# Accumulator banks handed out in pairs, one maximum over two heads, values split by one instruction each: a hybrid encoder trunk on one NeuronCore

## The chip, the core and the metric

The kernel runs on 1 core of one Trainium2 chip. The metric is device time in microseconds of one execution; before the change it is 1155.11 us, the median of 3 runs (1154.3 to 1155.8). The engines are TensorE (PE: matmuls and transposes), VectorE (DVE), ScalarE (ACT), GpSimd (POOL) and SyncE (SP, which here only starts transfers).

## What is computed

A two-layer encoder over 512 positions of 1024 channels, all in float32:

```python
h = layer_norm(x, ln_in_g, ln_in_b)
for l in range(2):
    a_in, b_q, b_k, b_v, c_in, d_cq, d_ckv, d_kr = split(h @ w_in[l])
    o_a = silu(layer_norm(depthwise_conv31(a * sigmoid(gate))))
    o_b = attention(rope(rms(q)), rope(rms(k)), v)      # 4 heads of 64, 2 for k and v
    o_c = u * (sgu_w @ layer_norm(sv) + sgu_b)          # c_in through gelu
    o_d = attention(q_full, k_full, v_d)                # 4 heads, 64 + 32 wide, low rank
    h = layer_norm(ALPHA * h + concat(o_a, o_b, o_c, o_d) @ w_out[l])
    up = depthwise_conv3(h @ ffn_w_up[l])               # 2 x 2816 wide
    h = layer_norm(ALPHA * h + (silu(up[:, :2816]) * up[:, 2816:]) @ ffn_w_down[l])
```

An attention is `softmax(q k^T * scale) v` over all 512 positions.

## The kernel before, in words

Every float32 operand of a product is split into a high part (rounded to fp32r) and a low part, the difference. A product is then three matmuls, high x high, high x low and low x high (`mm3`, line 733). `split` (line 739) makes the parts: ACT copies the high part, DVE (POOL for some weights) subtracts for the low part. Weights come from memory in chunks (`load`, line 668) and are split the same way; their tiles are `raw`, `wh` and `wl`. The normalised stream lies in `hh` and `hl`.

Sums are built in PSUM. There are two kinds of tiles for it, four of each: `acc` (method `acc`, line 659) and `wk`, each 128 partitions x 512 float32.

- In the attention, `att_scores` (line 1178) takes two `acc` tiles, one for each of two heads, and fills them by 6 matmuls in one group. `att_probs` (line 1187) takes the negated maximum of each head's scores on DVE (`max`) and then the exponential with its sum on ACT (`prob`). This is done for 2 x 4 query tiles in the B heads and as often in the D heads, in each layer. Then `att_transpose` and `att_pv` multiply the probabilities with the values.
- The values `bv` and `dv` are read from a `wk` tile in `b_evac` (line 1009) and `d_up` (line 1118): ACT copies the high part of each head, DVE subtracts for the low part, in the order in which the two heads' halves of a PSUM result need them.
- The up-projection `ffn` (line 1340) goes over 22 pairs of 128 columns. For pair `i`, `col_mm` (line 847) puts 24 matmuls, in four groups of 6, into the first tile (the part that goes through silu) and 24 into the second (its factor). Even pairs from 2 on take `wk` tiles, odd ones `acc` tiles. The first two pairs (`split_pairs`) take `acc` tiles and are done in halves of 256 columns. `up_pair` (line 1321) reads each tile three times: ACT with bias and scale (tile `y`), then two DVE `scalar_tensor_tensor` of 511 columns for the neighbours of the convolution. What follows (silu, product, split) reads no PSUM.
- The output projection and the down-projection are `residual` (line 1274): in each half of the columns four `acc` tiles, one for each 128 positions. The first chunks of weights go to all four in turn; the last chunk (in the second half the last four or five) is done for one tile after the other, and DVE adds each finished tile to `h`.

The order of the work is made before anything is issued. Each call on an engine is recorded (`record`, line 378) with the instructions that it must follow; `access` (line 417) works that out from the parts of a tile that are read and written. `place` (line 490) then plays the engines forward with a cost for each instruction (`cost`, line 445), free slots of each kind of tile (`SLOTS`) and priorities: the place in the program plus a number from the table `TUNE`. `issue` writes the instructions out in that order, and there the tile framework adds the waits that each instruction has in the built program:

```python
pool, n = self.pools[a.kind]
a.real_tile = pool.tile(a.full, a.dt, tag=f"{a.kind}{a.slot}", name=a.name, bufs=1)
```

All instructions are issued from one line (610, after the change 619), so rows are told apart by their tiles.

Of the kernel before, what the change touches and what calls it, by code (L numbers as in the profile page):

```python
# [9 lines left out]
F32 = mybir.dt.float32  # L10
# [6 lines left out]
P = 128  # L17
# [31 lines left out]
for _k in KEYS:  # L49
# [7 lines left out]
SLOTS = {"u": 69, "raw": 3, "acc": 4, "wk": 4, "s": 48}  # L57
# [14 lines left out]
TUNE = {'window': 334,  # L72
         'slack': 0.0,
         'spare': 1,
         'ahead': {'A': 6,
                   'B': 10,
                   'D': 10,
                   'U': 21,
                   'V': 12,
                   'C': 44,  # L80
                   'O': 5,
                   'F': 2,
                   'W': 6,
                   'W1': 35,
                   'W0': 15,
                   'C0': 42,
                   'A1': 17,
                   'V0': 17,
                   'C1': 42,
                   'F1': 6,  # L90
                   'A0': 30,
                   'B1': 34,
                   'D0': 9,
                   'F0': 5,
                   'B0': 27,
                   'V1': 28,
                   'U1': 32,
                   'U0': 40,
                   'D1': 5},
         'lead': {'A': 32,  # L100
                  'B': 14,
                  'D': 45,
                  'U': 73,
                  'V': 8,
                  'C': 0,
                  'O': 5,
                  'F': 37,
                  'W': 8,
                  'D1': 5,
                  'A0': 11,  # L110
                  'U1': 69,
                  'C1': 11,
                  'O1': 0,
                  'D0': 22,
                  'B1': 15,
                  'F1': 16,
                  'O0': 2,
                  'U0': 84,
                  'V1': 15,
                  'V0': 15,  # L120
                  'C0': 13,
                  'B0': 3,
                  'F0': 45,
                  'A1': 30,
                  'W0': 14,
                  'W1': 6},
         'rank': {'.0': 23,
                  '.1': -404,
                  '.3': -339,
                  'a0': 33,  # L130
                  'a1': 72,
                  'a_norm0': -14,
                  'b0': -1,
                  'b0.0': -212,
                  'b0.1': 256,
                  'b0.2': 81,
                  'b0.3': -477,
                  'b1': -618,
                  'b1.2': -365,
                  'b1.3': 59,  # L140
                  'b_att0': 142,
                  'b_att0.00': -455,
                  'b_att0.01': 19,
                  'b_att0.0n': 962,
                  'b_att0.10': -33,
                  'b_att0.1n': 49,
                  'b_att1': 24,
                  'b_att1.00': -25,
                  'b_att1.01': -10,
                  'b_att1.1n': 8,  # L150
                  'b_heads0': -527,
                  'b_heads0.0': 159,
                  'b_heads0.1': -3,
                  'b_heads1': 182,
                  'b_heads1.0': -174,
                  'b_heads1.1': -110,
                  'b_heads1.2': -4,
                  'b_rope0': -265,
                  'b_rope1': 794,
                  'c0': 78,  # L160
                  'c0.0': -15,
                  'c0.1': 6,
                  'c0.3': -638,
                  'c1': -66,
                  'c1.0': -131,
                  'c1.1': -9,
                  'c1.3': 150,
                  'c_norm0': 237,
                  'c_norm1': -16,
                  'c_sgu0': -22,  # L170
                  'c_sgu1': -283,
                  'conv0': 854,
                  'conv0.1': -86,
                  'conv1.0': -162,
                  'd0.0': 372,
                  'd0.2': -163,
                  'd1': 7,
                  'd1.0': -183,
                  'd1.1': 270,
                  'd1.2': 216,  # L180
                  'd1.3': -49,
                  'd_att0': -2,
                  'd_att0.20': 11,
                  'd_att0.21': 95,
                  'd_att0.2n': 135,
                  'd_att0.30': -186,
                  'd_att0.31': 5,
                  'd_att0.3n': 4,
                  'd_att1': -419,
                  'd_att1.20': 302,  # L190
                  'd_att1.21': -1797,
                  'd_att1.30': -317,
                  'd_att1.31': -134,
                  'd_att1.3n': 49,
                  'd_lat0': -141,
                  'd_norm1': 19,
                  'd_up1': -91,
                  'down0': -2632,
                  'down0.0': 365,
                  'down0.1': 5,  # L200
                  'down0.2': -346,
                  'down0.3': 3,
                  'down1': 13,
                  'down1.0': -52,
                  'down1.1': 1,
                  'down1.2': -16,
                  'down1.3': -54,
                  'ffn0': 194,
                  'ffn1': -7,
                  'out0': 12,  # L210
                  'out0.0': -4,
                  'out0.2': 243,
                  'out0.3': 221,
                  'out1.1': -12,
                  'out1.2': 40,
                  'out1.3': 34,
                  'tables0': -660,
                  'tables1': 62}}
# [104 lines left out]
class Sched:  # L323
# [121 lines left out]
    def cost(eng, method, args, kw, outs, ins):  # L445
# [27 lines left out]
        if eng == "ACT":  # L473
            from_psum = any(psum(v) for v in ins)
            return ((50.0 if from_psum else 94.0) + n / 1.2 + 72.0 * ptrs + (115.0 if "accum_out" in kw else 0.0),
                    118.0 if from_psum else 95.0, False)
# [3 lines left out]
        return 150.0 + n * (1.66 if narrow and n == 512 else 2.1), 40.0, True  # L480
# [141 lines left out]
class Kern:  # L622
    def __init__(self, ctx, tc, x, wst, sguw, pp, rows, tabs, incol, out):
# [26 lines left out]
        self.loaded = {}  # L650
# [8 lines left out]
    def acc(self):  # L659
        return self.s.tile("acc", [P, 512], F32, "acc")  # L660
# [348 lines left out]
    def b_evac(self, l):  # L1009
# [4 lines left out]
        def evac(t, ps):  # L1014
# [5 lines left out]
            v = self.unit([P, 2, P], FR, nm="bv")  # L1020
            pv = ps[:, 384:512].rearrange("p (h c) -> p h c", c=64)
            for i in range(2):
                s.ACT.activation(v[:, i, 64 * i:64 * i + 64], pv[:, i, :], AF.Copy)
            s.ACT.activation(y, pq, AF.Copy)
            for i in range(2):
                s.DVE.tensor_sub(v[:, i, 64 - 64 * i:128 - 64 * i], pv[:, i, :], v[:, i, 64 * i:64 * i + 64].bitcast(F32))
            self.bv.append(v)
            self.by.append(y)
        return evac

    def b_rope(self):

        s = self.s
# [497 lines left out]
```

## Time and profile before

| what | value |
|---|---|
| runs | 1154.3, 1155.8, 1155.11 us |
| profiled execution, device time | 1155.01 us |
| its span in the profile | 1153.2 us |
| instructions in the span | 15412 |
| mean granted clock of PE | 0.998 |

The span runs from the first to the last instruction that the profiler saw; the device time has a little more around it. A busy share is the time in which an engine had an instruction under way. Matmuls are pipelined, so one matmul's duration is longer than the step from its start to the next one's start. PEclk is the clock granted to PE as a share of 2.4 GHz. "idle before, releaser" gives the idle time of an engine just before an instruction and what ended it.

### The profile page before, as it was taken

How to read it: one execution, taken by the hardware profiler on the slowest of the kernel's cores; microseconds unless marked ns; L12 is line 12 of the kernel's file. 1: busy time of each engine (PE TensorE's matmuls, PEld its weight loads, DVE VectorE, ACT ScalarE, POOL GpSimd, SP SyncE). 2: the span in 40 equal slices, each digit the busy share in tenths (PEclk: the TensorE clock that was granted, in tenths of full speed). 3: DMA queues.
4: the chain of work that ended last, by engine and by line, in shares of the span. 5: the costliest groups of instructions: out<-in, count | busy, mean ns of one | idle time of the engine just before them, and what ended most of it. 6: DMA issues, size and time to landing. Idle time of an engine off the chain costs nothing.

```text
span 1153.2 us, 15412 instructions
## 1 busy us (share of the span) xinstructions
PE 1131.9 (98%) x5802; PEld 959.7 (83%) x5802; DVE 771.0 (67%) x1307; ACT 558.2 (48%) x1203; POOL 169.4 (15%) x203
## 2 busy tenths in 40 slices
PE   6999999999999999999999999999999999999997
PEld 5888888988888888888889877889888888888886
DVE  7799996776666755245667999777776656551425
ACT  5759794254444543224254679733564444431221
POOL 5324324100000001000112734320000000000002
PEclk9999999999999999999999999999999999999999
DMA  6520022233233532135232002122353223231311
GB/s 228 165 74 20 19 92 74 74 97 104 92 92 109 167 106 79 55 110 166 95 124 68 7 20 58 53 92 73 128 164 111 92 92 110 74 110 42 105 56 73
DMA packets 32041, 105.71 MB, mean 92 GB/s; under 512 B 3680, under 2 KB 4064, under 8 KB 31968
## 3 DMA queue, kind: packets, MB, share of 16 engines
q1 hardware_dynamic: 31968, 104.74, 27.7%
q8 instruction: 45, 0.74, 0.3%
q14 instruction: 28, 0.23, 0.1%
HBM read 102.63 MB, written 2.10 MB: 91 GB/s over the span
## 4 chain that ended last, share of the span: by engine, by line
PE 90%; ACT 5%; DVE 2%; DMA 1%; issue 1%; POOL 0%; SPq 0%; DVEq 0%; ACTq 0%
PE acc L610 55%; PE wk L610 35%; ACT prob L610 2%; ACT pth L610 1%; ACT wh L610 1%; DVE ptl L610 1%; ACT c L610 1%; DVE aconv L610 0%; DMA raw<-in_wst_dram 0%; DMA h<-in_x_dram 0%; ACT do L610 0%; DVE max L610 0%; DVE bo L610 0%; ACT mixh L610 0%; ACT bo L610 0%
## 5 line engine op out<-in xcount | busy, mean ns | idle before, releaser
L610 DVE TENSOR_TENSOR wl<-raw,wh 128x512 fp32r<-128x512 f32 (+1 forms) x264 | 171.6, 688 | 85.6 <-ACT wh L610 60.6
L610 ACT ACTIVATE wh<-raw 128x512 fp32r<-128x512 f32 (+2 forms) x310 | 176.1, 615 | 67.8 <-DMA raw<-in_wst_dram 60.8
L610 PE MATMUL acc<-hh,wh 128*128 128x512 f32 (+1 forms) x544 | 191.8, 353 | 0.0
L610 PE MATMUL acc<-hh,wl 128*128 128x512 f32 (+1 forms) x544 | 191.2, 352 | 0.0
L610 PE MATMUL acc<-hl,wh 128*128 128x512 f32 (+1 forms) x544 | 191.2, 352 | 0.0
L610 PE MATMUL wk<-hh,wh 128*128 128x512 f32 x320 | 124.5, 389 | 0.0
L610 PE MATMUL wk<-hl,wh 128*128 128x512 f32 x320 | 124.5, 389 | 0.0
L610 PE MATMUL wk<-hh,wl 128*128 128x512 f32 x320 | 124.5, 389 | 0.0
L610 PEld LDWEIGHTS acc<-hh,wl 128*128 128x128 f32 x544 | 102.8, 189 | 13.8
L610 PEld LDWEIGHTS acc<-hl,wh 128*128 128x128 f32 x544 | 102.9, 189 | 13.6
L610 PEld LDWEIGHTS acc<-hh,wh 128*128 128x128 f32 x544 | 102.9, 189 | 13.6
L610 POOL TENSOR_TENSOR vr<-ve,mhalf 128x1 f32<-128x1 f32 (+2 forms) x26 | 25.4, 977 | 534.6 <-DVE ve L610 534.5
L610 DVE SCALAR_TENSOR_TENSOR y<-acc,pp,y 128x511 f32<-128x511 f32 x96 | 71.6, 749 | 37.2 <-ACT y L610 35.4
L610 DVE TENSOR_TENSOR hl<-raw,hh 128x512 fp32r<-128x512 f32 x56 | 37.7, 689 | 84.3 <-ACT hh L610 84.2
L610 ACT ACTIVATE hh<-raw 128x512 fp32r<-128x512 f32 x56 | 34.9, 630 | 111.5 <-PE acc L610 93.5
L610 DVE SCALAR_TENSOR_TENSOR aconv<-aglu,pp,aconv 128x501 f32<-128x501 f32 (+14 forms) x120 | 86.7, 758 | 0.6
L610 PE MATMUL acc<-hl,fh 128*128 128x512 f32 x224 | 85.8, 383 | 0.0
L610 PE MATMUL acc<-hh,fh 128*128 128x512 f32 x224 | 85.7, 383 | 0.0
L610 PE MATMUL acc<-hh,fl 128*128 128x512 f32 x224 | 85.7, 382 | 0.0
L610 DVE SCALAR_TENSOR_TENSOR y<-wk,pp,y 128x511 f32<-128x511 f32 x80 | 60.0, 750 | 33.7 <-ACT y L610 31.9
L610 PE MATMUL wk<-wh,hh 128*128 128x512 f32 (+1 forms) x192 | 73.7, 384 | 0.0
L610 POOL TENSOR_TENSOR wl<-raw,wh 128x512 fp32r<-128x512 f32 (+1 forms) x46 | 59.8, 1320 | 91.6 <-ACT wh L610 58.3
(201 smaller groups left out, 2290.5 us busy)
## 6 DMA issues: line engine op xcount, KB each, us to landing
raw<-in_wst_dram SPq DMA_DIRECT2D x172, 512.0 KB, 3.5
row<-in_rows_dram SPq DMA_DIRECT2D x16, 256.0 KB, 5.0
raw<-in_wst_dram SPq DMA_DIRECT2D x8, 352.0 KB, 3.0
out_dram<-h SPq DMA_DIRECT2D x8, 256.0 KB, 2.0
h<-in_x_dram SPq DMA_DIRECT2D x3, 512.0 KB, 5.2
raw<-in_wst_dram SPq DMA_DIRECT2D x2, 384.0 KB, 3.8
h<-in_x_dram SPq DMA_DIRECT2D x2, 256.0 KB, 3.1
raw<-in_wst_dram SPq DMA_DIRECT2D x2, 256.0 KB, 3.1
```

What stands on the lines that cost most here:

```text
L610: f(*[a.real() if isinstance(a, View) else a for a in args], **{k: v.real() if isinstance(v, View) else v for k, v in kw.items()})
```

## The change

1. `acc` hands out halves: every second call makes one tile of 128 x 1024 and returns its first half, the next call returns the second half. `SLOTS` goes from 4 to 2 of them.
2. `att_probs` takes one maximum over both halves (128 x 2 x 512 to 128 x 2); the exponentials stay one a head.
3. The four 64-column parts of a pair of heads lie side by side as high, low, low, high, so one ACT copy writes both high parts and one DVE subtraction both low parts (`bv`; for `dv` both pairs of heads at once).
4. `cost` counts less for the sum beside an exponential and other amounts for POOL; the table `TUNE` (a window, a slack, how early chunks are loaded and split, ranks of sections) is set anew.

```diff
-SLOTS = {"u": 69, "raw": 3, "acc": 4, "wk": 4, "s": 48}
+SLOTS = {"u": 69, "raw": 3, "acc": 2, "wk": 4, "s": 48}
...
-TUNE = {'window': 334,
-         'slack': 0.0,
+TUNE = {'window': 528,
+         'slack': 62.7,
...
-            return ((50.0 if from_psum else 94.0) + n / 1.2 + 72.0 * ptrs + (115.0 if "accum_out" in kw else 0.0),
+            return ((50.0 if from_psum else 94.0) + n / 1.2 + 72.0 * ptrs + ((30.0 if n == 512 else 115.0) if "accum_out" in kw else 0.0),
...
     def acc(self):
-        return self.s.tile("acc", [P, 512], F32, "acc")
+
+        if self.acc_next is None:
+            pair = self.s.tile("acc", [P, 1024], F32, "acc")
+            self.acc_next = pair[:, 512:1024]
+            return pair[:, 0:512]
+        half, self.acc_next = self.acc_next, None
+        return half
...
-            v = self.unit([P, 2, P], FR, nm="bv")
+            v = self.unit([P, 4, 64], FR, nm="bv")
             pv = ps[:, 384:512].rearrange("p (h c) -> p h c", c=64)
-            for i in range(2):
-                s.ACT.activation(v[:, i, 64 * i:64 * i + 64], pv[:, i, :], AF.Copy)
+            s.ACT.activation(v[:, 0:4:3, :], pv, AF.Copy)
             s.ACT.activation(y, pq, AF.Copy)
-            for i in range(2):
-                s.DVE.tensor_sub(v[:, i, 64 - 64 * i:128 - 64 * i], pv[:, i, :], v[:, i, 64 * i:64 * i + 64].bitcast(F32))
-            self.bv.append(v)
+            s.DVE.tensor_sub(v[:, 1:3, :], pv, v[:, 0:4:3, :].bitcast(F32))
+            self.bv.append([v[:, 2 * i:2 * i + 2, :].rearrange("p a c -> p (a c)") for i in range(2)])
...
-            v = self.unit([P, 2, 2, P], FR, nm="dv")
+            v = self.unit([P, 2, 4, 64], FR, nm="dv")
...
+            hi = v[:, :, 0:4:3, :]
+            s.ACT.activation(hi, pv, AF.Copy)
+            s.DVE.tensor_sub(v[:, :, 1:3, :], pv, hi.bitcast(F32))
...
         m, ps = self.small([P, 2], nm="max"), []
+        s.DVE.tensor_reduce(m, sc[0].t.rearrange("p (h n) -> p h n", h=2), AX.X, ALU.max, negate=True)
         for j in range(2):
-            s.DVE.tensor_reduce(m[:, j:j + 1], sc[j], AX.X, ALU.max, negate=True)
             p = self.unit([P, S], nm="prob")
```

In instructions of the built program: PE keeps its 5804 rows; DVE has 32 maxima instead of 64, and 16 subtractions for `bv` and `dv` instead of 32; ACT has 16 copies for them instead of 32. POOL and SP keep theirs.

**The order on PE in the up-projection.** Layer 0, pair 5, with the waits of the built program; the number behind a name tells one buffer from another. Before, the last two matmuls of the first tile (`acc_671`), the first group of 6 into the second tile (`acc_672`) and the beginning of its second group:

```order
L610 MATMUL acc_671_3189<-hl_88,wh_676_3059 128x512
L610 MATMUL acc_671_3189<-hh_87,wl_677_3063 128x512
L610 MATMUL acc_672_3233<-hh_87,wh_679_3091 128x512 [waits PE_49,Activation_49]
L610 MATMUL acc_672_3233<-hl_88,wh_679_3091 128x512
L610 MATMUL acc_672_3233<-hh_87,wl_680_3101 128x512 [waits DVE_49]
L610 MATMUL acc_672_3233<-hh_87,wh_679_3091 128x512
L610 MATMUL acc_672_3233<-hl_88,wh_679_3091 128x512
L610 MATMUL acc_672_3233<-hh_87,wl_680_3101 128x512
L610 MATMUL acc_672_3233<-hh_87,wh_679_3091 128x512
L610 MATMUL acc_672_3233<-hl_88,wh_679_3091 128x512
L610 MATMUL acc_672_3233<-hh_87,wl_680_3101 128x512
L610 MATMUL acc_672_3233<-hh_87,wh_679_3091 128x512
```

With the change, from the last matmul into the first half of `acc_644` on: the first group of 6 into its second half, and the beginning of the second group:

```order
L619 MATMUL acc_644_3150<-hh_87,wl_649_2936 128x512
L619 MATMUL acc_644_3150<-hh_87,wh_651_2969 128x512
L619 MATMUL acc_644_3150<-hl_88,wh_651_2969 128x512
L619 MATMUL acc_644_3150<-hh_87,wl_652_2979 128x512
L619 MATMUL acc_644_3150<-hh_87,wh_651_2969 128x512
L619 MATMUL acc_644_3150<-hl_88,wh_651_2969 128x512
L619 MATMUL acc_644_3150<-hh_87,wl_652_2979 128x512
L619 MATMUL acc_644_3150<-hh_87,wh_651_2969 128x512 [waits DVE_49]
L619 MATMUL acc_644_3150<-hl_88,wh_651_2969 128x512
L619 MATMUL acc_644_3150<-hh_87,wl_652_2979 128x512
L619 MATMUL acc_644_3150<-hh_87,wh_651_2969 128x512
L619 MATMUL acc_644_3150<-hl_88,wh_651_2969 128x512
```

Before, the second tile's waits stand at its first use of a weight's high and low part. Now the first matmul of the second group waits for DVE; the count that it waits for is that of the first `y_655` row below. The first matmul of the third group, six rows on, waits for DVE again, for the count of the second `y_655` row.

**The order on DVE at the same place.** The subtractions for weights (`wl`) and the convolution of the pair. Before:

```order
L610 TENSOR_TENSOR wl_709_3231<-raw_705_3198,wh_708_3227 128x512 [waits Activation_49]
L610 SCALAR_TENSOR_TENSOR y_683_3240<-acc_671_3189,pp_89,y_683_3240 128x511 [waits Activation_49]
L610 SCALAR_TENSOR_TENSOR y_683_3240<-acc_671_3189,pp_89,y_683_3240 128x511 [waits DVE_49]
L610 TENSOR_TENSOR wl_712_3269<-raw_710_3242,wh_711_3259 128x512 [waits DMAHW0_49,Activation_49]
L610 TENSOR_TENSOR wl_714_3271<-raw_710_3242,wh_713_3267 128x512 [waits Activation_49]
L610 SCALAR_TENSOR_TENSOR y_684_3280<-acc_672_3233,pp_89,y_684_3280 128x511 [waits Activation_49]
```

With the change:

```order
L619 TENSOR_TENSOR wl_696_3192<-raw_692_3159,wh_695_3188 128x512 [waits Activation_49]
L619 SCALAR_TENSOR_TENSOR y_655_3200<-acc_644_3150,pp_89,y_655_3200 128x511 [waits Activation_49]
L619 SCALAR_TENSOR_TENSOR y_655_3200<-acc_644_3150,pp_89,y_655_3200 128x511 [waits DVE_49,PE_49]
L619 TENSOR_TENSOR wl_699_3229<-raw_697_3202,wh_698_3219 128x512 [waits DMAHW2_49,Activation_49]
L619 TENSOR_TENSOR wl_701_3231<-raw_697_3202,wh_700_3227 128x512 [waits Activation_49]
L619 SCALAR_TENSOR_TENSOR y_656_3240<-acc_644_3150,pp_89,y_656_3240 128x511 [waits Activation_49]
```

The rows stand in the same order. The second `y_655` row waits for PE too, for the count of the last matmul of the second half's second group. ACT's `y_655`, which the first one waits for, waits for PE in both kernels: before for the last matmul of its tile, now for the last one of the second half's first group.

**The order on DVE in the attention.** Layer 0, the third and fourth query tile of a D pair. Before, two heads' maxima with other work between them:

```order
L610 TENSOR_REDUCE max_397_1797<-acc_395_1754 128x1 [waits PE_49]
L610 TENSOR_TENSOR ptl_383_1801<-wk_381_1773,pth_382_1787 128x512 [waits Activation_49]
L610 TENSOR_TENSOR ptl_386_1812<-wk_384_1780,pth_385_1799 128x512 [waits Activation_49]
L610 TENSOR_TENSOR dl_436_1821<-wk_434_1747,dh_435_1803 96x512 [waits Activation_49]
L610 TENSOR_REDUCE max_397_1797<-acc_396_1755 128x1
L610 TENSOR_TENSOR ptl_390_1839<-wk_388_1807,pth_389_1827 128x512 [waits Activation_49]
L610 TENSOR_REDUCE max_402_1850<-acc_400_1789 128x1
```

With the change:

```order
L619 TENSOR_REDUCE max_382_1769<-acc_381_1745 128x2 [waits PE_49]
L619 TENSOR_TENSOR ptl_369_1790<-wk_367_1762,pth_368_1776 128x512 [waits Activation_49]
L619 TENSOR_TENSOR ptl_372_1801<-wk_370_1771,pth_371_1783 128x512 [waits Activation_49]
L619 TENSOR_TENSOR ptl_376_1805<-wk_374_1778,pth_375_1792 128x512 [waits Activation_49]
L619 TENSOR_TENSOR ptl_379_1814<-wk_377_1785,pth_378_1803 128x512 [waits Activation_49]
L619 TENSOR_REDUCE max_386_1822<-acc_385_1794 128x2 [waits PE_49]
```

One row now gives both heads' maxima, and both heads' exponentials stand behind it.

## Rows read from the trace of the kernel before

**Rows 1.** The page's first part: busy time, share of the span, instructions, by engine.

```profile
PE 1131.9 (98%) x5802; PEld 959.7 (83%) x5802; DVE 771.0 (67%) x1307; ACT 558.2 (48%) x1203; POOL 169.4 (15%) x203
```

**Rows 2.** The chain of work that ended last, shares of the span by engine.

```profile
PE 90%; ACT 5%; DVE 2%; DMA 1%; issue 1%; POOL 0%; SPq 0%; DVEq 0%; ACTq 0%
```

**Rows 3.** Stretches: busy PE, PEld, DVE, ACT, POOL (instructions), PEclk, DMA share, GB/s.

```profile
10.00:20.00 10.00, 7.46 (x32) 5.46 (x32) 7.63 (x15) 4.57 (x9) 8.69 (x8) 0.88 0.77 286
20.00:30.00 10.00, 10.00 (x51) 8.26 (x51) 9.69 (x20) 8.23 (x36) 3.30 (x6) 0.95 0.28 112
129.00:168.00 39.00, 36.56 (x243) 31.54 (x242) 37.26 (x75) 38.43 (x92) 15.59 (x13) 1.00 0.25 82
241.00:448.00 207.00, 207.00 (x915) 171.39 (x914) 135.08 (x198) 96.84 (x159) 3.72 (x4) 1.00 0.34 110
666.00:730.00 64.00, 61.06 (x393) 50.62 (x392) 61.27 (x113) 57.40 (x129) 19.41 (x22) 1.00 0.19 58
700.00:710.00 10.00, 8.32 (x53) 6.95 (x52) 9.14 (x19) 9.85 (x22) 6.30 (x6) 1.00 0.22 79
```

**Rows 4.** Timeline of an odd up-projection pair: start us, us, engine, line, operation.

```profile
256.66 0.39 PE L610 MATMUL acc<-hl,wh 128*128 128x512 f32 x1
...
256.88 0.39 PE L610 MATMUL acc<-hh,wl 128*128 128x512 f32 x1
...
257.11 0.39 PE L610 MATMUL acc<-hh,wh 128*128 128x512 f32 x1
...
257.31 0.78 ACT L610 ACTIVATE y<-acc,pp 128x512 f32<-128x512 f32 x1 [0.60 <-PE acc L610]
257.34 0.39 PE L610 MATMUL acc<-hl,wh 128*128 128x512 f32 x1
...
258.13 0.75 DVE L610 SCALAR_TENSOR_TENSOR y<-acc,pp,y 128x511 f32<-128x511 f32 x1 [0.53 <-ACT y L610]
```

**Rows 5.** Groups by line: busy us, mean ns of one, idle before.

```profile
L610 DVE SCALAR_TENSOR_TENSOR y<-acc,pp,y 128x511 f32<-128x511 f32 x96 | 71.6, 749 | 37.2 <-ACT y L610 35.4
...
L610 DVE TENSOR_REDUCE max<-acc 128x1 f32<-128x512 f32 x64 | 42.7, 681 | 0.2
...
L610 ACT ACTIVATE y<-acc,pp 128x512 f32<-128x512 f32 x48 | 37.4, 779 | 48.9 <-PE acc L610 48.8
...
L610 DVE SCALAR_TENSOR_TENSOR h<-h,acc 128x512 f32<-128x512 f32 (+1 forms) x32 | 21.7, 679 | 42.9 <-PE acc L610 42.9
...
L610 DVE TENSOR_TENSOR dv<-wk,dv 128x128 fp32r<-128x128 f32 x16 | 3.9, 281 | 0.6 <-POOL dk L610 0.6
...
L610 DVE TENSOR_TENSOR bv<-wk,bv 128x64 fp32r<-128x64 f32 x16 | 3.4, 221 | 10.3 <-ACT by L610 9.6 <-ACT bv L610 0.6
```

**Rows 6.** Timeline in the attention of layer 0, where PE waited for DVE and ACT.

```profile
144.97 0.69 DVE L610 TENSOR_TENSOR ptl<-wk,pth 128x512 fp32r<-128x512 f32 x1
...
145.71 0.39 PE L610 MATMUL wk<-pth,dv 128*128 128x256 f32 x1 [0.16 <-DVE ptl L610]
...
145.94 0.28 PE L610 MATMUL wk<-ptl,dv 128*128 128x256 f32 x1
...
146.05 0.28 PE L610 MATMUL wk<-pth,dv 128*128 128x256 f32 x1
...
146.95 0.20 ACT L610 ACTIVATION_READ_ACCUMULATOR prob<-acc,max 128x1 f32 x1
...
147.20 0.50 PE L610 MATMUL acc<-dh,dh 96*128 96x512 f32 x1 [0.52 <-ACT prob L610]
```

**Rows 7.** Timeline of PE near the start.

```profile
16.20 0.66 PE L610 MATMUL wk<-ident,h 128*128 128x128 f32 x4 [2.47 <-DVE h L610]
...
17.39 0.40 PE L610 MATMUL wk<-wh,hh 128*128 128x512 f32 x1
...
20.13 0.63 PE L610 MATMUL wk<-wh,hl 128*128 128x512 f32 x1
20.56 0.63 PE L610 MATMUL wk<-wh,hh 128*128 128x512 f32 x1
```

More of the change, by code (lines that the diff above doesn't have):

```diff
@@ new lines @@
+         'ahead': {'A': 21,
+                   'B': 9,
+                   'D': 4,
+                   'U': 18,
+                   'V': 10,
+                   'C': 51,
+                   'O': 25,
+                   'F': 36,
+                   'W': 1,
+                   'W1': 32,
+                   'W0': 19,
+                   'C0': 52,
+                   'A1': 10,
+                   'V0': 8,
+                   'C1': 37,
+                   'F1': 7,
+                   'A0': 26,
+                   'B1': 15,
+                   'D0': 16,
+                   'F0': 7,
+                   'B0': 40,
+                   'V1': 26,
+                   'U1': 30,
+                   'U0': 60,
+                   'D1': 5,
+                   'O1': 4,
+                   'O0': 5},
@@ new lines @@
+         'lead': {'A': 41,
+                  'B': 54,
+                  'D': 33,
+                  'U': 70,
+                  'V': 9,
+                  'C': 0,
+                  'O': 1,
+                  'F': 63,
+                  'W': 13,
+                  'D1': 20,
+                  'A0': 20,
+                  'U1': 69,
+                  'C1': 24,
+                  'O1': 1,
+                  'D0': 44,
+                  'B1': 19,
+                  'F1': 4,
+                  'O0': 5,
+                  'U0': 84,
+                  'V1': 0,
+                  'V0': 1,
+                  'C0': 15,
+                  'B0': 8,
+                  'F0': 39,
+                  'A1': 29,
+                  'W0': 19,
+                  'W1': 4},
@@ L479, in cost @@
         narrow = any(0 in v.arr.strides for v in ins)
-        return 150.0 + n * (1.66 if narrow and n == 512 else 2.1), 40.0, True
+        if n <= 8:
+            return 150.0, 40.0, True
+        return 320.0 + n * (1.4 if narrow and n == 512 else 1.8), 40.0, True
     LAT = {"PE": 55.0, "DVE": 35.0, "ACT": 35.0, "POOL": 78.0, "SP": 60.0}
@@ L649, in __init__ @@
         self.pp_in, self.tabs_in = pp, tabs
-        self.loaded = {}
+        self.loaded, self.acc_next = {}, None
     def unit(self, shape, dt=F32, nm="u"):
@@ L1157, in d_up @@
             self.dk[t] = k
-            v = self.unit([P, 2, 2, P], FR, nm="dv")
+            v = self.unit([P, 2, 4, 64], FR, nm="dv")
             pv = ps[:, 256:512].rearrange("p (a b c) -> p a b c", a=2, b=2)
-            for j in range(2):
-                hi = v[:, :, j, j * 64:j * 64 + 64]
-                lo = v[:, :, j, 64 - j * 64:128 - j * 64]
-                s.ACT.activation(hi, pv[:, :, j, :], AF.Copy)
-                s.DVE.tensor_sub(lo, pv[:, :, j, :], hi.bitcast(F32))
-            self.dv[t] = v
+            hi = v[:, :, 0:4:3, :]
+            s.ACT.activation(hi, pv, AF.Copy)
+            s.DVE.tensor_sub(v[:, :, 1:3, :], pv, hi.bitcast(F32))
+            self.dv[t] = [[v[:, a, 2 * i:2 * i + 2, :].rearrange("p a c -> p (a c)") for i in range(2)] for a in range(2)]
     def d_head(self, h):
@@ L1180, in att_scores @@
         sc = [self.acc() for _ in items]
+        assert self.acc_next is None and sc[0].t is sc[-1].t
         with self.s.group():
@@ L1257, in b_attention @@
                 rows = slice(kv * 64, kv * 64 + 64)
-                heads.append((self.bq[pr], self.bq[2], rows, [v[:, kv, :] for v in self.bv]))
+                heads.append((self.bq[pr], self.bq[2], rows, [v[kv] for v in self.bv]))
             self.attention(heads, o)
@@ L1268, in d_attention @@
                 q, k = self.d_head(pr * 2 + j)
-                heads.append((q, k, rows, [v[:, pr, j, :] for v in self.dv]))
+                heads.append((q, k, rows, [v[pr][j] for v in self.dv]))
             self.attention(heads, o)
```

236 lines of the change are left out of this document (96 added, 140 removed).

## The prediction

> **What bounds the kernel now.** I read the busy shares first: TensorE (PE) is busy for 1131.9 of 1153.2 us, VectorE (DVE) for 67%, ScalarE (ACT) for 48% [rows 1]. The chain that ended last says the same, 90% of it is PE [rows 2]. Then I read the span by stage. In the feed-forward up-projection of layer 0 (241 to 448 us) PE is busy for 207.00 of 207 us while DVE has 135 and ACT 97: PE never waits there, and anything that makes it wait is paid in full [rows 3]. In the attention stages (129 to 168 and 666 to 730 us) PE still shows 36.56 of 39 and 61.06 of 64 us, but DVE and ACT are as full: 37.26 and 38.43 of 39 us in the first [rows 3]. So there is little to win: PE's idle time in the two attention stages is 2.4 + 2.9 = 5.4 us, and work taken from DVE and ACT can buy back only that, and perhaps as much again of matmuls that started late inside PE's busy time.
>
> The profiled execution took 1155.01 us, the median of the three runs is 1155.11; I sum against 1155.0. A measurement of this kernel can tell about 0.2% (2.3 us) from no change.
>
> **What the change takes away.** One maximum over two heads replaces two, 32 times. A subtraction of 64 columns takes 0.221 us, of 128 columns 0.281, a maximum over 512 columns 0.681 [rows 5]: between the last two 0.40 us for 384 columns, 1.04 ns each. A maximum over 1024 columns is then 0.681 + 0.533 = 1.21 us, 0.15 less than two, 4.7 us in all on DVE. Merging the values' parts removes 8 + 8 instructions on ACT and as many on DVE; by the same fixed part of about 0.15 us each that is 2.4 us on DVE and about as much on ACT, spread over the evacuations of B and D, where PE does not wait. Nothing is removed from PE. These gains count only in the attention stages: I take 5 us, between nothing (the first Exp of each pair now starts 0.53 us later, which may eat it) and 10.
>
> **What the change adds: waits in PE's queue.** The four accumulator tiles of 512 columns (a bank each) become two tiles of 1024, and the built program orders work by tile: a read of the first half waits for the writes into the second half that stand before it, and the next write into the second half waits for that read. The order shows it. In the up-projection pair shown from layer 0, the second half gets 24 matmuls in four groups of 6. ACT's y (`up_pair`, bias and scale) reads the first half, and the PE count that it waits for is that of the last matmul of the second half's group 1. The first scalar_tensor_tensor of y on DVE waits for this ACT instruction. And the first matmul of group 2 now waits for DVE, for exactly that scalar_tensor_tensor. In the kernel before this matmul waits for nothing. So PE finishes group 1, stands still while ACT and DVE each do one instruction, runs group 2, and stands still again while DVE does the second scalar_tensor_tensor, which waits for the end of group 2 and for which group 3 waits. PE takes its matmuls in order, so nothing can slip in.
>
> The price of each such stop comes from rows:
> - A matmul starts 0.227 us after the last (256.66, 256.88, 257.11). The last matmul of a half starts at 256.88; ACT's y starts at 257.31, 0.43 later; it takes 0.78; DVE starts at 258.13, 0.04 after ACT's end, and takes 0.75 [rows 4]. All y instructions take these times: 779 and 749 ns on average [rows 5].
> - PE goes on 0.05 us after a DVE instruction that held it (144.97 + 0.69 = 145.66, then 145.71), and as long after an ACT instruction and its read of the accumulator (146.95 + 0.20 = 147.15, then 147.20). The second matmul after the stop comes 0.23 after the first, the third 0.11 after the second (145.71, 145.94, 146.05): about 0.11 us more [rows 6].
> - Stop behind ACT and one DVE instruction: 0.43 + 0.78 + 0.04 + 0.75 + 0.05 - 0.23 + 0.11 = 1.93 us. Behind one DVE instruction: 0.43 + 0.75 + 0.05 - 0.23 + 0.11 = 1.11. Behind ACT alone: 0.43 + 0.78 + 0.05 - 0.23 + 0.11 = 1.14. Behind both DVE instructions: 1.11 + 0.78 = 1.89.
>
> Counting all PE instructions of the changed program whose wait is for a reader of the same tile's other half gives 57: 50 for DVE, 7 for ACT; the kernel before has none.
> - 20 odd pairs of the up-projection (10 a layer), 41 waits. 17 pairs are as above, 1.93 + 1.11 = 3.04 each, 51.7 us. One stops for ACT and then for both DVE instructions (1.14 + 1.89 = 3.03), one for ACT and one DVE instruction (2.25), one for the three singly (3.36). Together 60.3 us.
> - The first two pairs of each layer (`split_pairs`, 256 columns a matmul), 9 waits: three times 2.25 and once 3.36, 10.1 us.
> - The residual sums, 7 waits: the second tile of a pair cannot be continued until DVE has added the first to h, an instruction of 0.68 us [rows 5]: 0.43 + 0.68 + 0.05 - 0.23 + 0.11 = 1.04, 7.3 us.
>
> In all 77.7 us on the engine that sets the end, with no cover: in these stages PE has no idle time to lose [rows 3]. Even with nothing for the restarts (57 x 0.11 = 6.3) it is 71. The other way, a wl split of about 0.69 us may stand before the awaited DVE instruction; DVE is busy 65% of that stage, so on average 0.22 us for each of the 50 waits, 11 us.
>
> **The rest.** Scores need both banks of a pair free, as the group of their matmuls did before; in `a_proj` a pair is read only when both halves are done. The weights' transfers have more time than before. The new ranks and window move the order, but of the idle time that they could remove there is little, as said. The clock stays granted in full: in 700 to 710 us PE was busy for 8.32 of 10 us and the clock was 1.00 [rows 3]; the changed up-projection would have PE busy for some 88%.
>
> Sum: 1155.0 + 77.7 - 5 = **1228 us**. Its own bounds: 1155 + 71 - 10 = 1216 and, with nothing gained, 1155 + 77.7 + 11 = 1244.
>
> **The rivals.**
> 1. *The waits are met before PE comes to them.* The trace has PE filling one accumulator bank at 257.34 while ACT reads another from 257.31 [rows 4], so nothing in the work itself asks for these waits. If the awaited counts were already reached when PE arrives, only the gain is left: 1155 - 5 = 1150 us. This decides once a stop costs less than 5 / 57 = 0.09 us. The Trainium skill, "PSUM — Partial Sum Buffer", section "PSUM bank collisions raise a hardware error", asks only that accesses be guarded by bank and quadrant; by that rule no wait is needed between the halves, which is this rival. Against it stands the order: each awaited instruction itself waits for the matmul just ahead of the waiting one, so it cannot be done in time. 4%.
> 2. *The clock falls as well.* After the start, PE idled 2.47 us before 16.20; its matmuls then went from 0.40 to 0.63 us with 0.43 between starts until 20.56 [rows 7], and the granted clock is 0.88 and 0.95 in two stretches of 10 us, 1.2 + 0.5 = 1.7 us lost [rows 3]. If each of the 18 stops of about 1.9 us did that, 31 us come on top: 1259. The Trainium skill, "TensorE: Matmul & The Clock Gate", section "Part 1: The HAM clock gate", says that 1.2 GHz is the default and activity releases it, so idle PE time can bring it back. The trace speaks against it here: the start had been sparse for 16 us, and the attention stages with idle time in many places kept 1.00. 6%.
> 3. *The attention stages get worse too.* If ACT has nothing to do while the longer maximum runs, 32 x 0.53 = 17 us are lost and the 5 not gained: 1250. ACT is busy for 38.43 of 39 us with other work in layer 0's stage, so most is covered. 5%.
>
> **How the numbers follow.** The forecast has 85%. The range runs from its lower bound 1216 to rival 3's 1250; left out are rivals 1 and 2 and the forecast's tails, below 2 in 10. Slower by over 0.2% are the forecast and rivals 2 and 3: 0.96. Rival 1 gives faster 0.03, and 0.01 for a gain that does not reach 2.3 us.
>
> **What would show it.** In the profile after: PE's busy share falls to about 92%; the up-projection stage of a layer grows by about 30 us, with ACT and DVE busy as long as before; PE idles some 1.7 us for DVE's y and then 0.8, ten times a layer, and the list of waits has rows of PE behind DVE y that the kernel before does not have; the chain that ended last gains ACT y and DVE y. The maximum shows 32 times at about 1.21 us. The forecast is wrong if PE still has no idle time in the up-projection, if single stops are far from 1.9 and 1.1 us, or if the granted clock falls below 1 there.

## The result, and the profile after

The change takes 1242.64 us (median of 4 runs, 1241.62 to 1243.52) against 1155.35 for the kernel before beside it: ratio 1.0754, 95% interval 1.0737 to 1.0771, 87.3 us slower. The forecast was 1228, its range 1216 to 1250. The profiled execution took 1241.62 us, its span is 1239.8.

Busy time, share of the span and instructions of each engine, and the chain that ended last by engine, after; they answer to [rows 1] and [rows 2]:

```profile
PE 1153.0 (93%) x5802; PEld 961.3 (78%) x5802; DVE 772.0 (62%) x1259; ACT 555.9 (45%) x1187; POOL 166.3 (13%) x203
...
PE 86%; DVE 6%; ACT 6%; issue 1%; DMA 0%; DVEq 0%; SPq 0%; ACTq 0%
```

PE falls from 98% to 93% of a longer span. 12% of the chain is now DVE and ACT, where it was 7%. The list of waits (us in total, times, longest) has rows that the kernel before does not have:

```profile
PEld acc L619 <- DVE y L619: 68.6, 43, 2.1
...
PE acc L619 <- DVE y L619: 51.9, 44, 1.7
...
PEld acc L619 <- DVE h L619: 8.7, 8, 1.2
...
PE acc L619 <- ACT y L619: 6.1, 7, 0.9
```

One odd pair of layer 0's up-projection, timeline of PE, ACT and DVE (start, us, engine; in brackets the idle time before and what ended it), the counterpart of [rows 4]:

```profile
295.08 0.39 PE L619 MATMUL acc<-hh,wl 128*128 128x512 f32 x1
295.51 0.78 ACT L619 ACTIVATE y<-acc,pp 128x512 f32<-128x512 f32 x1 [2.01 <-PE acc L619]
296.32 0.75 DVE L619 SCALAR_TENSOR_TENSOR y<-acc,pp,y 128x511 f32<-128x511 f32 x1 [1.94 <-ACT y L619]
...
297.12 0.50 PE L619 MATMUL acc<-hh,wh 128*128 128x512 f32 x1 [1.65 <-DVE y L619]
...
298.38 0.40 PE L619 MATMUL acc<-hh,wl 128*128 128x512 f32 x1
298.82 0.75 DVE L619 SCALAR_TENSOR_TENSOR y<-acc,pp,y 128x511 f32<-128x511 f32 x1 [1.75 <-PE acc L619]
...
299.62 0.50 PE L619 MATMUL acc<-hh,wh 128*128 128x512 f32 x1 [0.84 <-DVE y L619]
```

The last matmul of group 1 starts at 295.08, ACT follows 0.43 later, DVE 0.03 after ACT, PE 0.05 after DVE; six matmuls later the same with DVE alone. The chain of waits shows what a pair pays (start, us, what; an even pair stands before and behind it):

```profile
277.79 10.88 PE wk L619 x48
288.67 6.81 PE acc L619 x30
295.49 0.02 issue
295.51 0.79 ACT y L619
296.30 0.03 issue
296.32 0.76 DVE y L619
297.08 0.04 issue
297.12 1.67 PE acc L619 x6
298.80 0.03 issue
298.82 0.76 DVE y L619
299.58 0.04 issue
299.62 3.02 PE acc L619 x12
302.64 10.88 PE wk L619 x48
```

The odd pair takes 302.64 - 288.67 = 13.97 us, an even one 10.88: 3.09 more, 3.04 forecast. The 18 odd pairs that the trace separates whole take 13.97 to 14.39 us, 3.09 over 10.88 in the middle.

Where the 87.3 us lie is read from the starts of PE's matmuls in the profiled execution. F0 and F1 are the first matmuls with 256 columns of layer 0's and of layer 1's up-projection. "to F0" is the start of F0; "first pairs" go from F0 or F1 to the first matmul with 512 columns into `wk` behind it; "rest of 0" goes from there to the first matmul of layer 1 from `hh` into `wk`, "layer 1 to F1" from there to F1; "rest of 1" ends with PE's last matmul. All later runs are in the same table.

| kernel | median us | to F0 | first pairs, 0 | rest of 0 | layer 1 to F1 | first pairs, 1 | rest of 1 |
|---|---|---|---|---|---|---|---|
| before | 1155.35 | 216.01 | 24.75 | 339.00 | 203.07 | 24.75 | 338.58 |
| the change | 1242.64 | 223.39 | 29.35 | 372.49 | 202.38 | 31.97 | 373.19 |
| e12 single banks, order of the change | 1159.01 | 219.90 | 24.78 | 339.00 | 201.30 | 24.76 | 338.58 |
| e1 the change, halves crosswise | 1175.11 | 222.62 | 25.38 | 343.14 | 204.69 | 26.92 | 341.11 |
| e11 as e1, other finishing order | 1169.64 | 225.30 | 25.64 | 339.17 | 206.46 | 25.04 | 338.65 |
| e8 as e1, old ranks | 1174.13 | 220.13 | 26.40 | 341.76 | 207.78 | 26.38 | 342.72 |
| e2 single banks, new ranks | 1172.89 | 228.00 | 24.78 | 339.84 | 209.07 | 24.74 | 338.58 |
| e3 pairs, old ranks | 1247.20 | 222.36 | 29.25 | 373.05 | 213.27 | 28.26 | 372.88 |
| e4 merged values alone | 1160.68 | 216.04 | 24.76 | 338.99 | 208.15 | 24.74 | 338.58 |
| e5 as e4, order of before | 1154.21 | 215.98 | 24.75 | 339.00 | 202.67 | 24.74 | 338.58 |
| e6 crosswise pairs alone | 1170.79 | 220.76 | 26.40 | 342.04 | 205.69 | 26.39 | 341.12 |
| e7 as e6, one maximum | 1175.89 | 222.91 | 26.41 | 343.35 | 206.24 | 26.41 | 341.11 |
| e9 as e6, other finishing order | 1164.85 | 222.71 | 25.57 | 339.09 | 204.68 | 25.57 | 338.68 |
| e10 as e9, one maximum | 1169.02 | 225.63 | 25.56 | 339.08 | 206.70 | 25.57 | 338.66 |

The four feed-forward stages of the change are 4.6 + 33.5 + 7.2 + 34.6 = 79.9 us longer. The rest is nearly all ahead of layer 0's up-projection: 7.4 us.

### The profile page after: what moved, and what is told of

Same layout as the page of the kernel before. It is cut to its first block, busy times and chain, and to the rows that moved or that the text cites. A ratio compares the mean times of both kernels' runs of the same rounds, so it can differ in the third digit from the quotient of the medians.

```text
span 1239.8 us, 15346 instructions
## 1 busy us (share of the span) xinstructions
PE 1153.0 (93%) x5802; PEld 961.3 (78%) x5802; DVE 772.0 (62%) x1259; ACT 555.9 (45%) x1187; POOL 166.3 (13%) x203
## 4 chain that ended last, share of the span: by engine, by line
PE 86%; DVE 6%; ACT 6%; issue 1%; DMA 0%; DVEq 0%; SPq 0%; ACTq 0%
PE acc L619 53%; PE wk L619 33%; DVE y L619 3%; ACT y L619 2%; ACT prob L619 2%; DVE h L619 1%; ACT pth L619 1%; DVE max L619 0%; ACT c L619 0%; DVE bst L619 0%; DVE aconv L619 0%; ACT dc L619 0%; DMA incol<-in_incol_dram 0%; DVE ptl L619 0%; ACT bo L619 0%
## 5 line engine op out<-in xcount | busy, mean ns | idle before, releaser
L619 PE MATMUL acc<-hh,wh 128*128 128x512 f32 (+1 forms) x544 | 198.3, 365 | 57.5 <-DVE y L619 51.3
L619 DVE TENSOR_TENSOR wl<-raw,wh 128x512 fp32r<-128x512 f32 (+1 forms) x264 | 175.2, 698 | 92.8 <-ACT wh L619 62.0
L619 DVE SCALAR_TENSOR_TENSOR aconv<-aglu,pp,aconv 128x499 f32<-128x499 f32 (+14 forms) x120 | 88.6, 774 | 0.6
L619 ACT ACTIVATE y<-acc,pp 128x512 f32<-128x512 f32 x48 | 37.3, 776 | 102.0 <-PE acc L619 94.1
```

What stands on the lines that cost most here:

```text
L619: f(*[a.real() if isinstance(a, View) else a for a in args], **{k: v.real() if isinstance(v, View) else v for k, v in kw.items()})
```

## The experiments

The theory: a tile of two banks puts a read of one half and the next write into the other half in line, and PE stops. Against it stood the new ranks, the one maximum, and pairs as such.

**The tile alone (e12).** Planned as the change, each pair then made of two tiles:

```diff
-                    a.real_tile = pool.tile(a.full, a.dt, tag=f"{a.kind}{a.slot}", name=a.name, bufs=1)
+                    if a.kind == "acc":
+                        a.real_tile = Banks([pool.tile([P, 512], a.dt, tag=f"acc{a.slot}{c}", name=f"{a.name}_{c}", bufs=1) for c in range(2)])
+                    else:
+                        a.real_tile = pool.tile(a.full, a.dt, tag=f"{a.kind}{a.slot}", name=a.name, bufs=1)
...
-        s.DVE.tensor_reduce(m, sc[0].t.rearrange("p (h n) -> p h n", h=2), AX.X, ALU.max, negate=True)
+        om = s.DVE.tensor_reduce(m, sc[0].t.rearrange("p (h n) -> p h n", h=2), AX.X, ALU.max, negate=True)
+        om.calls = [("tensor_reduce", (m[:, j:j + 1], sc[j], AX.X, ALU.max), {"negate": True}) for j in range(2)]
```

(`Banks` gives the tile of the half that is asked for.)

> The change with the order of every engine kept instruction by instruction as the change has it, but each accumulator pair is two tiles of one bank (so a read of one no longer stands in line with writes into the other), and two maxima of 512 columns are issued one behind the other where the one of 1024 stood. Theory (the tile of two banks makes the loss, the order does not): the up- and down-projections fall back to 339 and 338.6 us and the first pairs to 24.8, which is 79.9 us less, and up to 5 more because the exponentials need not wait for the longer maximum: 1157 to 1164 us; what is left above 1155 is the price of the new order alone. Rival (the order by the new ranks makes the loss): above 1200.

Measured: 1159.01 us, ratio to before 1.0034 (1.0022 to 1.0046). Busy shares, and layer 0's up-projection as a stretch of 207 us (columns as in [rows 3]):

```profile
PE 1133.2 (98%) x5802; PEld 960.7 (83%) x5802; DVE 771.3 (67%) x1291; ACT 555.7 (48%) x1187; POOL 166.7 (14%) x203
...
245.00:452.00 207.00, 207.00 (x915) 171.39 (x914) 132.73 (x193) 94.75 (x155) 3.28 (x4) 1.00 0.32 104
```

PE is busy for all 207 us again, as in [rows 3]. The sequences of instructions on PE, ACT and POOL are the change's own, and DVE's differs in the maxima alone. So the order does not make the loss. Tiles of two banks, with the one maximum that needs them, cost 1242.64 - 1159.01 = 83.6 us; the order alone costs 3.9.

**Crosswise halves (e1).** The change as it is, but tiles filled one after the other come from different pairs:

```diff
+    def crossed(self):
+        x, y = [self.s.tile("acc", [P, 1024], F32, "acc") for _ in range(2)]
+        return [[t[:, 512 * j:512 * j + 512] for t in (x, y)] for j in range(2)]
...
-            ps = [[(0, 512, self.acc())] for _ in range(NT)]
+            halves = self.crossed()
+            ps = [[(0, 512, halves[t // 2][t % 2])] for t in range(NT)]
...
-        pss = [[self.acc(), self.acc()] for _ in range(split_pairs)]
+        pss = self.crossed()
...
-                ps = [self.acc(), self.acc()]
+                if i % 4 == 3:
+                    halves = self.crossed()
+                ps = halves[i % 4 == 1]
```

> The change with everything kept (pairs, one maximum, merged values, new ranks), but the halves handed out crosswise: in the odd pairs of the up-projection, in its first two pairs and in the residual sums, two tiles that are filled one after the other now lie in different accumulator pairs. What is computed stays the same. Theory (PE stops because a read of one half and the next write into the other half of the same tile are put in line): the stops in these three places go, the stage from the first full even pair to the end of layer 0's down-projection is 339 us again instead of 372.5, and the whole comes to 1242.6 minus 75 to 85, 1158 to 1168 us. Rival A (the new ranks and window make the order worse): at least 1225. Rival B (accumulators in pairs are slow for PE whatever the order of reads): unchanged, about 1240.

Measured: 1175.11 us, 67.5 less than the change, but above the range of 1158 to 1168. The chain in layer 0's first and second full pairs:

```profile
242.17 5.99 PE acc L619 x48
248.16 10.91 PE wk L619 x48
259.07 10.88 PE acc L619 x48
```

Odd pairs take 10.88 us again: with the same two-bank tiles, PE does not stop if the other half's readers are done. Rivals A and B fall. What is left in the feed-forward stages (0.6 + 4.1 + 2.2 + 2.5 = 9.4 us) lies mostly at the start of the down-projections, where PE stops for 1.85 us in each layer; e9 and e11 come back to it.

**Ranks and single banks (e2, e3).** e2 is the change with `SLOTS` at 4 accumulators of 512 columns and two maxima, e3 the change with the old costs and `TUNE`:

```diff
-SLOTS = {"u": 69, "raw": 3, "acc": 2, "wk": 4, "s": 48}
+SLOTS = {"u": 69, "raw": 3, "acc": 4, "wk": 4, "s": 48}
```

> The change with accumulators of one bank each and two maxima again; merged values, new costs and new ranks stay. Theory (stops): no stops, so 1150 to 1165; above 1157 if the 7 us that layer 0 lost ahead of its up-projection come from the new order, below if they come from pairs or from the one maximum. Rival A (ranks): 1225 or more. Rival C (the one maximum delays the exponentials enough to make most of the loss): about 1155 as well, which is why the next run and the one before stand beside it.

> The change with the costs and the table of ranks of the kernel before; pairs, one maximum and merged values stay. The built program has 54 waits of PE for the other half of a tile instead of 57. Theory (stops): 1225 to 1240, a stage of an up-projection as long as with the change. Rival A (ranks): 1150 to 1158.

Measured: e2 1172.89, e3 1247.20. With old ranks the stops are there (54 waits of the 57), and the feed-forward stages are 76.4 us longer than before; without pairs they are gone under the new ranks too. But e2 came out above its range: planned for single banks by the new ranks, the attention stages lose 12.0 and 6.0 us. These ranks, set for pairs, do not suit single banks. For the change itself they gain 1247.20 - 1242.64 = 4.6 us.

**Merged values (e4, e5).** e4 is the kernel before with only the merged values of the diff above. e5 has the same instructions, but the planner sees two of each kind:

```diff
+    def merged(self, ops, k, call):
+        for o in ops:
+            o.calls = []
+        ops[k].calls = [call]
...
+            self.merged(oa, 0, ("activation", (v[:, 0:4:3, :], pv, AF.Copy), {}))
+            self.merged(od, 1, ("tensor_sub", (v[:, 1:3, :], pv, v[:, 0:4:3, :].bitcast(F32)), {}))
```

> The kernel before with only the merged values (16 instructions less on ACT and 16 less on DVE). Theory: on both engines this lies beside other work, 1153 to 1155.5. Rival D (the merged copy has to finish for both heads before the subtraction starts, and the values come later): 1157 or more.

> The kernel before with merged values as in the run of merged values alone (1160.7 us), but the order is planned with the two instructions of each kind as before and only one of them issued: the copy where the first copy stood, the subtraction where the second stood. Every other instruction of every engine stands where it stood before. Theory (the 5.4 us of the run of merged values alone came from the order that the planner made anew, all of it in layer 1 between the start of its attention and its up-projection): 1153 to 1155.5. Rival (a merged instruction itself delays the values): 1158 or more, and again in layer 1.

Measured: e4 1160.68 us, ratio 1.0049 (1.0033 to 1.0066), slower where I expected nothing; e5 1154.21, ratio 0.9993 (0.9984 to 1.0001). 32 fewer instructions are worth less than can be measured, and the 5 us of e4 are the order that the planner made when their cost fell away, all of them in layer 1 ahead of its up-projection (208.15 against 203.07). In that stage the granted clock of e4 was 0.50 from 708 to 711 us, where the kernel before has 1.00, so a part of the 5 us is the clock.

**One maximum (e6, e7, e9, e10).** e6 is the kernel before with pairs handed out crosswise, two maxima, nothing else. e7 issues one maximum where the first of the two stood; e9 and e10 are the same two, with the plain `acc` in the residual sums and another finishing order:

```diff
+        self.merged(om, 0, ("tensor_reduce", (m, sc[0].t.rearrange("p (h n) -> p h n", h=2), AX.X, ALU.max), {"negate": True}))
...
-            for t in range(NT):
+            for t in (0, 2, 1, 3):
                 ts = slice(t * P, (t + 1) * P)
```

> The kernel before with accumulators in pairs handed out crosswise in the up-projection and the residual sums, and nothing else of the change: two maxima, values as before, old costs and ranks. Theory: the stops are gone but for the two places where the crosswise run still lost time (first pairs, and the start of the down-projection: together 9.4 us in that run); in the attention two banks that come free together instead of one by one cost nothing that the planner cannot place elsewhere: 1157 to 1167. Rival (pairs as such are dear in the attention, because the next scores now wait for both heads' exponentials): 1168 or more, with the loss between the first scores and the up-projection of each layer.

> The run of crosswise pairs alone, with one maximum over both heads issued where the first of the two stood, and every other instruction of every engine in the same order. Theory of the prediction (4.7 us less on DVE, worth between 0 and that much on PE): 0 to 5 us below the run of crosswise pairs alone. Rival (the first exponential starts 0.53 us later and PE is behind it): 3 to 17 us above it.

> The run of crosswise pairs alone, but the residual sums take their four tiles from the pairs in the plain way (first and second position from the first pair) and finish them in the order 0, 2, 1, 3, so that a tile is read while the other pair is written. The residual sums then no longer need both pairs free before they can start. Theory (of the 15.9 us that crosswise pairs alone lost, those at the start of the down-projections, 3.0 and 2.5, and part of layer 0's 4.2 in the attention come from that need, since the first matmul of the output projection started 7 us later than in the kernel before): 1158 to 1166, with the up- and down-projection of layer 0 at 339 to 340 us again. Rival (pairs as such are dear in the attention): 1166 to 1171, nothing gained there.

> The run with the other finishing order, with one maximum issued where the first of the two stood; the order of every engine is otherwise the same. The price of the one maximum once more, in another order of the work. If it comes from the exponentials that start later: 3 to 7 us above the run beside it, with ACT waiting longer for the maximum. If the 5.1 us of the first such pair belonged to that order alone: within 2 us of the run beside it. The prediction's term: 0 to 5 us below it.

Measured: e6 1170.79 (1.0136), above its range and where its rival stood (1168 or more); e7 1175.89 (1.0181, 1.0167 to 1.0195); e9 1164.85 (1.0081, 1.0066 to 1.0096); e10 1169.02 (1.0117, 1.0102 to 1.0132). Groups of e6, e7, e9 and e10 in turn (busy, mean ns | idle before and what ended most of it), the exponentials and the maxima of e6 and e7 first:

```profile
L610 ACT ACTIVATE prob<-acc,max 128x512 f32<-128x512 f32 x64 | 44.2, 692 | 3.5 <-DVE max L610 3.1
...
L610 DVE TENSOR_REDUCE max<-acc 128x1 f32<-128x512 f32 x64 | 42.8, 681 | 2.4 <-ACT prob L610 2.1 <-PE acc L610 0.2
```

```profile
L610 ACT ACTIVATE prob<-acc,max 128x512 f32<-128x512 f32 x64 | 44.1, 691 | 6.1 <-DVE max L610 5.6
...
L610 DVE TENSOR_REDUCE max<-acc 128x2 f32<-128x1024 f32 x32 | 38.8, 1214 | 0.7 <-PE acc L610 0.6
```

```profile
L610 ACT ACTIVATE prob<-acc,max 128x512 f32<-128x512 f32 x64 | 44.2, 693 | 3.8 <-DVE max L610 3.4
```

```profile
L610 ACT ACTIVATE prob<-acc,max 128x512 f32<-128x512 f32 x64 | 44.0, 690 | 6.8 <-DVE max L610 6.5
```

The one maximum takes 1.21 us as forecast and DVE saves 4.0 us, yet with everything else in place the kernel is 5.1 us slower, and 4.2 in the other order. ACT waits 2.5 and 3.1 us longer for the maximum: the first exponential of each pair starts later, ACT is as full there as PE [rows 3], and PE is behind it. That is the mechanism of my third rival, at less than a third of its 17 us. Not all of the 5.1 and 4.2 us is shown to be this wait. In the profiled executions e7 is 4.0 us longer than e6, and 1.3 of them lie in the rest of layer 0, where at the start of the down-projection the granted clock was 0.50 from 471 to 474 us in e7 and 1.00 in e6. The few executions with the same mean granted clock are 3.3 us apart in both pairs (e7 1175.3 and e6 1172.0 at 0.996, e10 1167.1 and e9 1163.8 at 0.999).

e9 also shows where most of the 8.9 us went that e6 lost in the feed-forward stages: with the finishing order changed, the residual sums no longer need both pairs before they start, the rest of each layer is 339.09 and 338.68 again, and 1.8 of the 8.9 us are left. The attention does not come back, however: 6.7 us to F0 and 1.6 in layer 1 are still lost. Whether the coupling of two banks or the order that the planner makes with it costs that was not separated.

**The change with the stops taken out (e8, e11).** e8 is e1 with the old costs and ranks; e11 is the change with crosswise up-projection and the finishing order 0, 2, 1, 3.

> The change with halves handed out crosswise, and with the costs and ranks of the kernel before. Theory (the stops and the order of the attention stages add up and do not touch each other): the run with old ranks, 1247.2, less what handing out crosswise took from the change, 67.5: 1175 to 1185 us. Rival (the old ranks suit this form once the stops are gone): 1155 to 1165.

> The change with all its parts and its new ranks, halves handed out crosswise in the up-projection, and residual sums finished in the order 0, 2, 1, 3. Theory: the crosswise run of the change was 1175.1, its down-projections lost 4.1 and 2.5 us, so 1165 to 1171. It is slower than the kernel before by what the one maximum (about 5) and the coupling of two banks in the attention cost. Rival (with the stops gone the change gains in the attention after all): below 1155.

Measured: e8 1174.13, 0.9 below its range and level with e1, so that without the stops the new ranks gain nothing; e11 1169.64 (ratio 1.0120, 1.0104 to 1.0137), 73.0 us less than the change. The feed-forward stages of e11 are those of the kernel before to within 1.4 us in all, and it is still 14 us slower, in the attention stages. No version beat the kernel before; e5 is level with it.

## Why the prediction was right, and where its terms were off

- **What bounds the kernel:** PE without idle time in the up-projection, so any wait there is paid in full. e12 gives the 207 of 207 us back, and the 79.9 us appear one for one in the total. Right.
- **The waits exist and cannot be met in time** (against rival 1): PE idles 1.65 and 0.84 us at just the two matmuls that the order names. Right. The Trainium skill, "PSUM — Partial Sum Buffer", section "PSUM bank collisions raise a hardware error", asks for a guard by bank and quadrant, or more simply by bank; e12, whose tiles are one bank each, agrees: with the same order PE is busy for 207 of 207 us, so the waits came from the tile of two banks.
- **The price of a stop:** 1.93 + 1.11 = 3.04 a pair, 3.09 measured. 20 pairs by 3.09 are 61.8, 60.3 forecast. Of the 11 us for a `wl` split ahead of the awaited instruction little came: in the pair shown DVE had been idle for 1.94 us when ACT was done, and one of the 18 pairs is more than 0.1 us above the middle.
- **The first pairs:** 10.1 forecast, 4.6 + 7.2 = 11.8 measured. Layer 0 has two stops of 2.25 (4.5, 4.6 measured), layer 1 one of 2.25 and one of 3.36 (5.6, 7.2 measured); about 1.5 of the 1.6 more are the clock, see rival 2. **The residual sums:** seven stops counted; PE idles behind DVE's `h` eight times, 0.34 to 0.78 us each. Two of the eight (563.67 and 1170.78 us) are first matmuls of the second half's sums, which I had not counted: a pair comes free only when both its halves have been read. The four feed-forward stages come to 74.6 forecast (60.3 + 10.1 + 4 x 1.04) and 79.9 measured, 5.3 short.
- **"I take 5 us, between nothing and 10" for the attention:** this step failed, in its sign. The merged values are worth nothing measurable (e5), the one maximum costs 4.2 to 5.1 us (e7, e10), some 3.3 where the clock is the same. I had counted instructions saved on DVE, where the latency from the scores to the first exponential sets ACT, and through it PE. The lower bound should have been below nothing, and by my own third rival.
- **"The new ranks and window move the order, but of the idle time that they could remove there is little":** right on what they could win, but they can lose. The order alone is 3.9 us slower (e12). Outside the feed-forward stages the forecast was 3 x 1.04 - 5 = -1.9 us; measured are 3.9 for the order and 83.6 - 79.9 = 3.7 for the rest, 9.5 us apart. With the 5.3 above this is the distance of 14.6 us from 1228 to 1242.64, to 0.2.
- **Rival 2, the clock:** "The clock stays granted in full" holds for the full pairs of the up-projection and fails once in its first pairs. A stretch of 235 us of layer 0 (columns as in [rows 3]) has the clock in full:

```profile
253.00:488.00 235.00, 212.47 (x915) 170.10 (x914) 131.96 (x191) 94.98 (x155) 3.28 (x4) 1.00 0.29 91
```

In layer 1's first pairs three stops follow each other with six matmuls of 256 columns between them; the timeline of PE, and the stretches behind them, in which the clock is 0.50 (1.2 GHz):

```profile
845.47 0.39 PE L619 MATMUL acc<-hh,wh 128*128 128x256 f32 x1 [0.87 <-ACT y L619]
...
847.36 0.39 PE L619 MATMUL acc<-hh,wh 128*128 128x256 f32 x1 [0.91 <-DVE y L619]
...
849.18 0.39 PE L619 MATMUL acc<-hh,wh 128*128 128x256 f32 x1 [0.84 <-DVE y L619]
```

```profile
849.00:850.00 1.00, 0.82 (x6) 0.82 (x7) 0.13 (x1) 0.63 (x1) 0.00 (x0) 0.87 0.00 0
850.00:851.00 1.00, 1.00 (x6) 1.00 (x6) 0.00 (x0) 0.58 (x1) 0.00 (x0) 0.50 0.00 0
...
852.00:853.00 1.00, 1.00 (x7) 1.00 (x7) 1.00 (x2) 0.24 (x1) 0.00 (x0) 0.50 0.00 0
853.00:854.00 1.00, 1.00 (x10) 1.00 (x9) 0.97 (x3) 0.00 (x0) 0.00 (x0) 0.92 0.00 0
```

Sixteen matmuls start 0.21 us apart there and not 0.12, which is about 1.5 us. So the rival's mechanism did appear in the up-projection, once, not 18 times for 31 us. It is the prediction's own sign against it ("if the granted clock falls below 1 there"), too small to move the result.
- **Where luck came in:** 1242.64 lies below the forecast's own upper bound of 1244, but not for the bound's reasons. The 11 us of `wl` splits in it hardly came; the order, the one maximum and the clock, which the sum had at nothing or as a gain, filled their place.

## What to carry to other kernels

When two buffers are joined into one tile so that one instruction can read both, look up in the built program what the tile is waited for as a whole: a read of one half then stops the writes into the other, and on the engine that sets the end each stop costs the reader's whole latency, some 1.0 to 1.9 us here, 57 times. Handing out the halves so that neighbours in time lie in different tiles removes that without giving up the joint tile. And a merged instruction is worth its saved time only if nothing waits for its first half, and only if the order around it is kept: a planner that sees other costs can lose more (5 us in e4) than the instruction saves, so price the instruction in the old order first.

## What the runs showed of the hardware that was not expected

The clock of PE fell at a second place of the change, in layer 0's attention. PE, timeline, and the stretches of 1 us that follow (columns as in [rows 3], the clock is the third number from the right):

```profile
145.16 0.73 PE L619 MATMUL acc<-dh,dh 96*128 96x512 f32 x2 [3.10 <-ACT prob L619]
...
146.71 3.53 PE L619 MATMUL wk<-ident,prob 128*128 128x128 f32 x16
```

```profile
145.00:146.00 1.00, 0.84 (x4) 0.71 (x5) 0.59 (x2) 0.95 (x4) 0.00 (x0) 1.00 0.00 0
...
147.00:148.00 1.00, 1.00 (x7) 1.00 (x6) 1.00 (x1) 0.70 (x2) 0.27 (x1) 0.50 0.00 0
...
149.00:150.00 1.00, 1.00 (x8) 1.00 (x6) 0.87 (x2) 0.74 (x2) 0.00 (x0) 0.50 0.00 0
150.00:151.00 1.00, 1.00 (x7) 0.82 (x5) 0.73 (x2) 0.77 (x3) 0.00 (x0) 1.00 0.00 0
```

PE had idled 3.10 us behind ACT; the clock then was 0.50 (1.2 GHz) from 147 to 150 us and full again in the next stretch, while the stops of 1.65 and 0.84 us, two in an odd pair, left it at 1.00. The 16 transposes took 3.53 us there. In the kernel before this stage kept 1.00 [rows 3]; in e12, which has the order of the change, it was 0.50 from 144 to 147 us behind stops of 1.92 and 0.68 us, so this fall comes with the order and not with the pairs. The Trainium skill, "TensorE: Matmul & The Clock Gate", section "Part 1: The HAM clock gate", has idleness bring the slow clock back; the trace agrees at this stop of 3.10 us and at the three of under 1 us in layer 1's first pairs, and shows nothing of it at the stops of the full pairs. ACT's part in that stop is a table load of 1.28 us just ahead of the first of the two exponentials that PE waits for; the kernel before has the two loads of this stage at 114.09 and 134.71 us, the change at 134.39 and 141.85:

```profile
141.85 1.28 ACT L619 ACT_TABLE_LOAD   x1
143.15 0.69 ACT L619 ACTIVATE prob<-acc,max 128x512 f32<-128x512 f32 x1
```
